# Scan systems stored in DRAM as the scan reads them, one load a step for six; the second branch's gates kept on chip

## The chip, the cores and the metric

One core of one Trainium2 chip. The metric is the time of one execution in device microseconds (us). Below, PE is TensorE, DVE is VectorE, ACT is ScalarE, POOL is GpSimd and SP is SyncE, which issues most of the DMAs. ACT issues a few DMAs too, from its own queue. In the profile, SP's transfers are DMA queue q1 and ACT's are q10.

## The reference

One layer over 256 latent tokens `x` with 256 context tokens `ctx`, all widths 2048, in float32. Two branches read the same modulated input: latent attention (MLA, 8 heads) and a bidirectional chunked gated DeltaNet (8 heads, chunks of 64 tokens). Their outputs are projected, gated, summed and projected again; a ConvGLU of width 5504 follows.

```python
(lq_a, lkv_a, lk_r, ldq, ldk, ldv, ldz, lda, ldb, lga, lgb) = split_columns(
    modulate(rmsnorm(x, norm_mix[l]), sh1, sc1) @ w_in[l])
...
m = jnp.where(strict, jnp.einsum('bhnid,bhnjd->bhnij', kb, k) * decay, 0.0)
rhs = jnp.concatenate([v * beta, kb * jnp.exp(gc)[..., None]], axis=-1)
sol = lax.linalg.triangular_solve(m + jnp.eye(c, dtype=m.dtype), rhs,
                                  left_side=True, lower=True, unit_diagonal=True)
...
def step(s, inp):
    v_new = u_c - jnp.einsum('bhcd,bhde->bhce', w_c, s)
    s_next = s * g_c + jnp.einsum('bhcd,bhce->bhde', k_c, v_new)
    o = jnp.einsum('bhcd,bhde->bhce', q_c, s) + jnp.einsum('bhcj,bhje->bhce', a_c, v_new)
...
merged = jax.nn.sigmoid(gate_mla) * (y_mla @ w_o_mla) + jax.nn.sigmoid(gate_dn) * (y_dn @ w_o_dn)
return merged @ w_out
```

What the change touches are the unit triangular 64 x 64 systems `m + I`. Each chunk has one for every head and direction. The kernel inverts them and the scan multiplies by the inverse.

## The kernel before

Nearly all time goes into matmuls of weights, which are read from DRAM once, in tiles of 128 x 1024 (512 KB, named `raw`) or 128 x 2048 (`wt`, 1 MB). For precision, each half of a tile is split into two parts: ACT casts it to `whi` (line 121) and DVE subtracts to get `wlo` (line 122); PE then runs over both. So a `raw` that lands late delays ACT's cast, DVE's subtraction and PE in turn. Over most of the program the order of PE's instructions is written out by hand; ACT, DVE and SP are put in order by a scheduler that estimates when each operand is ready.

Every DMA, on SP or on ACT, takes one of eight semaphores (`DMAHW0` to `DMAHW7`) in turn and first waits for the DMA that held the same one eight places before, whichever queue that was on. A waiting DMA holds all that stands behind it on its queue.

The stages that matter here, in order of time:

- Start (0 to some 60 us): `cv`, `sel`, `vecs`, then `xl` (the latent tokens) and `xc` (the context) in four loads each, then the adaLN weights `wt` and `raw<-in_wadab` and the first projection's `gr`. PE computes norms (`scp`, `pss`), the adaLN vectors (`amp`) and the first projections (`fp`).
- `inverse` (lines 818 to 843, about 425 to 455 us in the profile): DVE inverts the 32 x 32 diagonal blocks of all systems in the tile `ux`, and SP stores them to the DRAM tensor `Xq` in 12 stores of 32 rows of 4 KB: the first block transposed (`xt`), the first and the second.
- `off_diagonal` (lines 846 to 882, 480 to 630 us): eight steps `q` compute the 32 x 32 blocks off the diagonal from `xd<-Xq` and `uo`; ACT copies the result to `uo` and stores it to `Xo`, one store a step.
- Gates: `gate_tiles` multiplies by `wgm` and `wgd` (`gtp`), and `gate_fin` stores the tanh (`zx`) of each of 2 x 16 tiles to the DRAM tensor `Gs` from ACT's queue. `branch` loads them again, four tiles a load (`gt`), when the branch's output (`brp`) has to be gated.
- `scan` (line 1224 on, about 715 to 925 us): eight steps, each of which needs the system of its chunk in the tile `tt0` or `tt1`. `load_system` (line 1241) fills it by six loads, of 256 rows of 128 bytes each, from `Xq` and `Xo`; the quarter that stays zero was set once by POOL. PE runs the rest of the gate tiles of `wgd` and the first branch's projections (`womla`) between the steps' own products (`yp`, `sp_`, `kp`, `op`); these weights are loaded on SP's queue behind the loads of the scan.

Of the kernel before, what the change touches and what calls it, by code (L numbers as in the profile page):

```python
# [8 lines left out]
F32 = mybir.dt.float32  # L9
# [44 lines left out]
def hybrid_block(ctx: ExitStack, tc: tile.TileContext, io, dbg=None):  # L54
# [44 lines left out]
    ones = const.tile([P, 1], F32, name="ones")  # L99
    dve.memset(ones, 1.0)  # L100
    onesr = const.tile([P, P], F32R, name="onesr")
    dve.tensor_copy(onesr, ones.broadcast_to([P, P]))
# [547 lines left out]

    Xq = dram.tile([3, 32, 4, 32, 32], F32, name="Xq")
    Xo = dram.tile([32, 4, 32, 32], F32, name="Xo")
    As = dram.tile([4, P, 8, 64], F32, name="As")
# [164 lines left out]
    def inverse():  # L818
# [20 lines left out]
        for g in range(4):  # L839
            gs = slice(32 * g, 32 * g + 32)  # L840
            for n, x in enumerate((xt, X[:, 0], X[:, 1])):
                sync.dma_start(Xq[n, :, g], x[gs])
        yield 1000
        pI.close()

    def off_diagonal():
# [7 lines left out]
        def load(q):  # L854
            rs = slice(4 * q, 4 * q + 4)
            uo = pi.tile([P, 4, 32], F32, tag="uo", name="uo", bufs=2)
            sync.dma_start(uo, Uo[:, :, rs].rearrange("g j r i -> (g j) r i"))
            xd = pi.tile([P, 2, 4, 32], F32, tag="xd", name="xd", bufs=2)
            for n in range(2):
                sync.dma_start(xd[:, n], Xq[2 * n, rs].rearrange("r g j c -> (g j) r c"))  # L860
            return uo, xd
# [3 lines left out]
        for q in range(8):  # L865
# [14 lines left out]
            act.copy(uo, ip)  # L880
            act.dma_start(Xo[4 * q : 4 * q + 4].rearrange("r g c i -> (g c) r i"), uo)
            yield OC / 2
# [7 lines left out]
    def gate_fin(ps, out, fin):  # L890
        x = pz.tile([P, T], F32, tag="zx", name="zx")
        gather(ps, P, x)
        if fin is None:
            act.activation(x, x, AF.Tanh, scale=0.5)
        else:
            fin(x)
        act.dma_start(out, x)

# [285 lines left out]
    fill.finish()  # L1184
    gates = gate_tiles([("wgd", f, Gs[1, :, f], None) for f in range(KD)])
    for _ in range(4 * GD0):
# [8 lines left out]
    pd2 = pD.enter_context(pool_("pd2", 2))  # L1195
    YM = hp.tile([P, HEADS, 2, T], F32R, tag="x16", name="YM")
    yraw = pd.tile([P, HEADS, T], F32, tag="o", name="yraw")
    sync.dma_start(yraw, Ys)
# [4 lines left out]
    def branch(w, wh, f, ymat, out):  # L1203

        if f % 4 == 0:
            gt = pd2.tile([P, 4, T], F32, tag="gt", name="gt")
            sync.dma_start(gt, Gs[wh, :, f : f + 4])
            gts[wh] = gt
        W = load_w(io[w][f])
        ps = psm.tile([P, 512], F32, tag="mm", name="brp")  # L1210
# [6 lines left out]
        dve.scalar_tensor_tensor(out=ox, in0=ps[:, :T], scalar=0.5, in1=ox, op0=ALU.mult, op1=ALU.add)  # L1217
        dve.scalar_tensor_tensor(out=out, in0=gts[wh][:, f % 4], scalar=1.0, in1=ox, op0=ALU.add, op1=ALU.mult)
        yield 1300
# [4 lines left out]
    def scan():  # L1224
# [4 lines left out]
        av = ps1.tile([P, HEADS, 64], F32, name="av")  # L1229
        for n in range(2):  # L1230
            pool.memset(TTv[n], 0.0)
        half_ = [slice(0, 64), slice(64, 128)]
# [9 lines left out]
        def load_system(n):  # L1242
            st, tt = steps[n], TTv[n % 2]
            for d in range(2):
                for r, c, x in ((0, 0, Xq[1]), (32, 32, Xq[2]), (0, 32, Xo)):
                    rs, cs = slice(64 * d + r, 64 * d + r + 32), slice(c, c + 32)
                    n = 16 * d + 2 * st
                    sync.dma_start(tt[rs, :, cs], x[n : n + 2].rearrange("a g c i -> c (a g) i"))
            return tt
# [359 lines left out]
```

## Time and profile before

| | |
|---|---|
| median of 3 runs | 1796.3 us (1796.25 to 1796.43) |
| profiled execution | 1796.66 us, of which the span from the first to the last instruction is 1794.8 us |
| granted TensorE clock, mean | 0.988 |
| busy: PE, DVE, ACT, POOL | 97%, 75%, 53%, 2% of the span |
| DMA | 419.79 MB in 191493 packets, 57248 of them under 512 B |

The profile is of one execution. Its page gives the busy time of each engine, the DMA queues and the groups of instructions; the views that are asked of the trace give rows by stretch of time (busy time of each engine in it, mean granted clock, the share of the 16 DMA engines that was busy, GB/s), the instructions of one engine in order of time with the idle time ahead of each and what ended it, the waits by engine, and the chain of work that ended last. A row such as `SPq L1248` is a DMA issued by SP at line 1248.

### The profile page before, as it was taken

The numbers are of one execution on the slowest core, as the hardware profiler recorded it, in microseconds if no ns is written. First come the engines' busy times: TensorE is split into PE (matmuls) and PEld (weight loads), VectorE is DVE, ScalarE is ACT, GpSimd is POOL, SyncE is SP. The second block draws the span as 40 slices with busy tenths as digits, with TensorE's granted clock in tenths as the row PEclk, the third lists the DMA queues.
The fourth block names the chain that finished last, engine by engine and source line by source line (L and its number), as shares of the span: only waits on it lengthen the run. The fifth ranks groups of instructions, "written<-read, shape, count | busy, mean of one in ns | idle before, by whom it ended". The sixth has DMA issues, their size and how long they took to land.

```text
span 1794.8 us, 34114 instructions
## 1 busy us (share of the span) xinstructions
PE 1740.9 (97%) x12957; PEld 1504.6 (84%) x12957; DVE 1353.9 (75%) x2692; ACT 944.5 (53%) x1962; POOL 42.1 (2%) x49
## 2 busy tenths in 40 slices
PE   7999999999999999899999989999999999999999
PEld 6787888887888888687878878888888888888888
DVE  4687899879677777576789889887788888755554
ACT  3334544444567666564655546555555555544443
POOL 0000010000000000000010000000000000000000
PEclk9999999999899999999999989999999999999999
DMA  9982788773778767888957966777677777666663
GB/s 383 399 319 89 207 241 241 228 213 104 220 241 260 229 213 249 279 308 309 317 166 240 327 234 224 244 229 229 190 224 226 225 225 225 184 199 199 198 199 122
DMA packets 191493, 419.79 MB, mean 234 GB/s; under 512 B 57248, under 2 KB 97312, under 8 KB 188896
## 3 DMA queue, kind: packets, MB, share of 16 engines
q1 hardware_dynamic: 164144, 402.38, 69.0%
q10 hardware_dynamic: 27184, 15.23, 2.8%
q8 instruction: 102, 1.67, 0.4%
q14 instruction: 63, 0.52, 0.1%
HBM read 388.57 MB, written 28.84 MB: 233 GB/s over the span
## 4 chain that ended last, share of the span: by engine, by line
PE 70%; issue 10%; DMA 9%; DVE 6%; ACT 3%; POOL 1%; SPq 0%; POOLq 0%; DVEq 0%; ACTq 0%
PE fps L68 25%; PE dps L68 13%; PE mmp L68 9%; PE gtp L68 7%; PE fp L68 4%; DMA rawa<-in_wada 4%; DVE wlo L122 2%; PE brp L68 2%; DMA raw<-in_wadab 1%; PE amp L68 1%; DVE rawa L279 1%; DMA raw<-in_wgd 1%; ACT whi L121 1%; PE op L68 1%; DMA raw<-in_wz 1%
## 5 line engine op out<-in xcount | busy, mean ns | idle before, releaser
L122 DVE TENSOR_TENSOR wlo<-raw,whi 128x512 fp32r<-128x512 f32 (+1 forms) x940 | 632.6, 685 | 220.4 <-ACT whi L121 212.1
L121 ACT CAST whi<-raw 128x512 fp32r<-128x512 f32 (+1 forms) x940 | 574.3, 619 | 425.2 <-PE dps L68 113.7
L68 PE MATMUL fps<-H,whi 128*128 128x512 f32 x1376 | 475.1, 394 | 1.7 <-DVE H L1446 1.7
L68 PE MATMUL fps<-H,wlo 128*128 128x256 f32 x1376 | 372.3, 281 | 0.3 <-DVE wlo L122 0.3
L68 PEld LDWEIGHTS fps<-H,whi 128*128 128x128 f32 x1376 | 253.7, 189 | 53.3 <-issue 2.0
L68 PEld LDWEIGHTS fps<-H,wlo 128*128 128x128 f32 x1376 | 259.8, 189 | 7.8 <-DVE wlo L122 0.7
L68 PE MATMUL gtp<-h,whi 128*128 128x512 f32 x640 | 235.1, 404 | 7.4 <-ACT whi L121 7.1
L68 PE MATMUL mmp<-h,whi 128*128 128x512 f32 x640 | 227.1, 397 | 0.0
L68 PE MATMUL dps<-GB,whi 128*128 128x512 f32 (+1 forms) x595 | 195.7, 378 | 0.0
L279 DVE CUSTOM_DVE_ANT_0 rawa<-rawa,sch 128x1024 f32<-128x1024 f32 x128 | 155.8, 1220 | 45.5 <-DMA rawa<-in_wada 41.9
L68 PE MATMUL gtp<-h,wlo 128*128 128x256 f32 x640 | 176.0, 285 | 4.4 <-DVE wlo L122 4.2
L68 PE MATMUL mmp<-h,wlo 128*128 128x256 f32 x640 | 176.0, 281 | 0.6 <-DVE wlo L122 0.6
L68 PE MATMUL dps<-GB,wlo 128*128 128x256 f32 x560 | 154.1, 280 | 0.0
L68 PEld LDWEIGHTS gtp<-h,whi 128*128 128x128 f32 x640 | 121.8, 192 | 34.1 <-ACT whi L121 9.5
L68 PEld LDWEIGHTS mmp<-h,whi 128*128 128x128 f32 x640 | 119.0, 188 | 24.7 <-issue 0.4
L68 PEld LDWEIGHTS gtp<-h,wlo 128*128 128x128 f32 x640 | 122.9, 192 | 11.9 <-DVE wlo L122 7.5
L68 PEld LDWEIGHTS dps<-GB,whi 128*128 128x128 f32 x595 | 109.2, 188 | 21.1
L68 PEld LDWEIGHTS mmp<-h,wlo 128*128 128x128 f32 x640 | 120.3, 188 | 3.9 <-DVE wlo L122 1.3
L68 PEld LDWEIGHTS dps<-GB,wlo 128*128 128x128 f32 x560 | 105.1, 188 | 0.6
L68 PE MATMUL fp<-h,gh 128*128 128x256 f32 (+1 forms) x448 | 85.1, 290 | 2.5 <-ACT h L68 1.7
L68 PEld LDWEIGHTS fp<-h,gh 128*128 128x128 f32 (+1 forms) x448 | 69.4, 189 | 7.6 <-issue 4.1
L517 ACT COPY fx<-fps 128x256 f32<-128x256 f32 x86 | 31.8, 372 | 65.4 <-PE fps L68 65.3
(566 smaller groups left out, 2525.4 us busy)
## 6 DMA issues: line engine op xcount, KB each, us to landing
rawa<-in_wada SPq DMA_DIRECT2D x128, 512.0 KB, 4.7
raw<-in_wgate SPq DMA_DIRECT2D x82, 512.0 KB, 4.3
raw<-in_wval SPq DMA_DIRECT2D x82, 512.0 KB, 4.6
raw<-in_wdown SPq DMA_DIRECT2D x80, 512.0 KB, 4.3
wt<-in_wadas SPq DMA_DIRECT2D x16, 1024.0 KB, 10.8
raw<-in_wadab SPq DMA_DIRECT2D x32, 512.0 KB, 9.2
raw<-in_wgm SPq DMA_DIRECT2D x32, 512.0 KB, 4.7
raw<-in_wgd SPq DMA_DIRECT2D x32, 512.0 KB, 6.1
```

Source lines behind the costliest of these rows:

```text
L68: i = f(*a, **k)
L121: act.copy(hi, raw)
L122: dve.tensor_tensor(out=lo, in0=raw, in1=hi, op=ALU.subtract)
L279: dve.tensor_tensor_reduce(out=w, in0=w, in1=sch, scale=1.0, scalar=0.0, op0=ALU.mult, op1=ALU.add, accum_out=parts[:, h, j : j + 1])
L517: act.copy(out, ps[:M, T:])
```

## The change

- A DRAM tensor `Tt` holds every system as the scan reads it: 128 rows (64 for each direction), 16 chunks and turns, 4 heads, 64 columns. `load_system` becomes one load of 128 rows of 2 KB.
- Its zero quarter is written at the start of the program by two stores from a zeroed tile `none`, on ACT's queue: 2048 pieces of 128 bytes each.
- `inverse` no longer stores the first block untransposed to `Xq` (12 stores become 8) and stores both diagonal blocks to `Tt` in 16 stores of 512 pieces of 128 bytes, on SP.
- `off_diagonal` stores its result to `Tt` in four stores a step on SP (32 in all), where there was one to `Xo` on ACT's queue.
- POOL's two zeroings of `tt0` and `tt1` go.
- The 14 gate tiles of `wgd` that are computed inside the scan stay on chip in a new tile `gk` (14 KB a partition); their 14 stores to `Gs` go, and of the four `gt` loads of 512 KB for the second branch one of 256 KB is left.
- `dynamic_dma_scratch_size=1024` makes the room for `gk`; addresses of other tiles move.

```diff
@@ -98,6 +98,8 @@
     make_identity(nc, ident)
     ones = const.tile([P, 1], F32, name="ones")
     dve.memset(ones, 1.0)
+    none = const.tile([P, 32], F32, name="none")
+    pool.memset(none, 0.0)
     onesr = const.tile([P, P], F32R, name="onesr")
     dve.tensor_copy(onesr, ones.broadcast_to([P, P]))
     half = const.tile([P, 1], F32, name="half")
@@ -648,8 +650,10 @@
     Ud = dram.tile([4, 32, 2, 32, 32], F32, name="Ud")
     Uo = dram.tile([4, 32, 32, 32], F32, name="Uo")
 
-    Xq = dram.tile([3, 32, 4, 32, 32], F32, name="Xq")
-    Xo = dram.tile([32, 4, 32, 32], F32, name="Xo")
+    Xq = dram.tile([2, 32, 4, 32, 32], F32, name="Xq")
+    Tt = dram.tile([P, 16, 4, 64], F32, name="Tt")
+    for d in range(2):
+        act.dma_start(Tt[64 * d + 32 : 64 * d + 64, :, :, 0:32].rearrange("c s g j -> c (s g) j"), none[:32].unsqueeze(1).broadcast_to([32, 64, 32]))
     As = dram.tile([4, P, 8, 64], F32, name="As")
     conv = mid.tile([P, 24, 3], F32, name="conv")
     dve.tensor_scalar(out=conv, in0=off["dn_conv"].rearrange("p (f w) -> p f w", w=3), scalar1=0.5, scalar2=None, op0=ALU.mult)
@@ -838,8 +842,13 @@
         act.copy(xt, X[:, 0].rearrange("p c j -> p j c"))
         for g in range(4):
             gs = slice(32 * g, 32 * g + 32)
-            for n, x in enumerate((xt, X[:, 0], X[:, 1])):
+            for n, x in enumerate((xt, X[:, 1])):
                 sync.dma_start(Xq[n, :, g], x[gs])
+        for g in range(4):
+            for d in range(2):
+                for b in range(2):
+                    rs = slice(64 * d + 32 * b, 64 * d + 32 * b + 32)
+                    sync.dma_start(Tt[rs, :, g, 32 * b : 32 * b + 32].rearrange("c s j -> s c j"), X[32 * g + 16 * d : 32 * g + 16 * d + 16, b])
         yield 1000
         pI.close()
 
@@ -857,7 +866,7 @@
             sync.dma_start(uo, Uo[:, :, rs].rearrange("g j r i -> (g j) r i"))
             xd = pi.tile([P, 2, 4, 32], F32, tag="xd", name="xd", bufs=2)
             for n in range(2):
-                sync.dma_start(xd[:, n], Xq[2 * n, rs].rearrange("r g j c -> (g j) r c"))
+                sync.dma_start(xd[:, n], Xq[n, rs].rearrange("r g j c -> (g j) r c"))
             return uo, xd
 
         ahead = load(0)
@@ -878,7 +887,9 @@
                 if n == 0:
                     yield OC / 2
             act.copy(uo, ip)
-            act.dma_start(Xo[4 * q : 4 * q + 4].rearrange("r g c i -> (g c) r i"), uo)
+            for g in range(4):
+                dst = Tt[64 * (q // 4) : 64 * (q // 4) + 32, 4 * (q % 4) : 4 * (q % 4) + 4, g, 32:64]
+                sync.dma_start(dst, uo[32 * g : 32 * g + 32])
             yield OC / 2
         pI.close()
 
@@ -888,13 +899,15 @@
     pz = ctx.enter_context(pool_("pz", 3))
 
     def gate_fin(ps, out, fin):
-        x = pz.tile([P, T], F32, tag="zx", name="zx")
+        kept = isinstance(out, int)
+        x = gk[:, out] if kept else pz.tile([P, T], F32, tag="zx", name="zx")
         gather(ps, P, x)
         if fin is None:
             act.activation(x, x, AF.Tanh, scale=0.5)
         else:
             fin(x)
-        act.dma_start(out, x)
+        if not kept:
+            act.dma_start(out, x)
 
     def gate_tiles(jobs):
 
@@ -1182,7 +1195,7 @@
         pass
     inv.finish()
     fill.finish()
-    gates = gate_tiles([("wgd", f, Gs[1, :, f], None) for f in range(KD)])
+    gates = gate_tiles([("wgd", f, Gs[1, :, f] if f < GD0 else f - GD0, None) for f in range(KD)])
     for _ in range(4 * GD0):
         next(gates)
     pC.close()
@@ -1194,6 +1207,7 @@
     pd = pD.enter_context(pool_("pd", 1))
     pd2 = pD.enter_context(pool_("pd2", 2))
     YM = hp.tile([P, HEADS, 2, T], F32R, tag="x16", name="YM")
+    gk = pd.tile([P, KD - GD0, T], F32, name="gk")
     yraw = pd.tile([P, HEADS, T], F32, tag="o", name="yraw")
     sync.dma_start(yraw, Ys)
     split(yraw, YM[:, :, 0], YM[:, :, 1])
@@ -1202,10 +1216,12 @@
 
     def branch(w, wh, f, ymat, out):
 
-        if f % 4 == 0:
+        if f % 4 == 0 and (f == 0 or not wh):
             gt = pd2.tile([P, 4, T], F32, tag="gt", name="gt")
-            sync.dma_start(gt, Gs[wh, :, f : f + 4])
+            n = GD0 if wh else 4
+            sync.dma_start(gt[:, :n], Gs[wh, :, f : f + n])
             gts[wh] = gt
+        gate = gk[:, f - GD0] if wh and f >= GD0 else gts[wh][:, f % 4]
         W = load_w(io[w][f])
         ps = psm.tile([P, 512], F32, tag="mm", name="brp")
         for k in range(HEADS):
@@ -1215,7 +1231,7 @@
         ox = pd2.tile([P, T], F32, tag="ox", name="ox")
         act.activation(ox, ps[:, T:], AF.Copy, scale=0.5)
         dve.scalar_tensor_tensor(out=ox, in0=ps[:, :T], scalar=0.5, in1=ox, op0=ALU.mult, op1=ALU.add)
-        dve.scalar_tensor_tensor(out=out, in0=gts[wh][:, f % 4], scalar=1.0, in1=ox, op0=ALU.add, op1=ALU.mult)
+        dve.scalar_tensor_tensor(out=out, in0=gate, scalar=1.0, in1=ox, op0=ALU.add, op1=ALU.mult)
         yield 1300
 
     gts = {}
@@ -1227,8 +1243,6 @@
         jit = ps1.tile([P, 6, 1024], F32, name="jit")
         TTv = [ps1.tile([P, HEADS, 64], F32, name=f"tt{n}") for n in range(2)]
         av = ps1.tile([P, HEADS, 64], F32, name="av")
-        for n in range(2):
-            pool.memset(TTv[n], 0.0)
         half_ = [slice(0, 64), slice(64, 128)]
         S = ps1.tile([P, HEADS, 2, P], F32, name="S")
         steps = (4, 5, 6, 7, 0, 1, 2, 3)
@@ -1241,11 +1255,7 @@
 
         def load_system(n):
             st, tt = steps[n], TTv[n % 2]
-            for d in range(2):
-                for r, c, x in ((0, 0, Xq[1]), (32, 32, Xq[2]), (0, 32, Xo)):
-                    rs, cs = slice(64 * d + r, 64 * d + r + 32), slice(c, c + 32)
-                    n = 16 * d + 2 * st
-                    sync.dma_start(tt[rs, :, cs], x[n : n + 2].rearrange("a g c i -> c (a g) i"))
+            sync.dma_start(tt, Tt[:, 2 * st : 2 * st + 2].rearrange("p a g j -> p (a g) j"))
             return tt
 
         def load_ke(n):
@@ -1598,7 +1608,7 @@
     import concourse.bacc as bacc
     from concourse.bass_utils import run_bass_kernel_spmd
 
-    nc = bacc.Bacc("TRN2", target_bir_lowering=False, num_devices=1)
+    nc = bacc.Bacc("TRN2", target_bir_lowering=False, num_devices=1, dynamic_dma_scratch_size=1024)
     arrays = {f"in_{n}": v for n, v in host(inputs).items()}
     io = {n[3:]: nc.dram_tensor(n, v.shape, mybir.dt.from_np(v.dtype), kind="ExternalInput").ap() for n, v in arrays.items()}
     io["out"] = nc.dram_tensor("out_0", (KD, P, T), F32, kind="ExternalOutput").ap()
```

The order of the instructions on the queues changes with it. ACT at the start of the program, before (`cv`, `sel` are small inputs, `cth` and `sq` the first arithmetic):

```order
L304 DMA cv<-in_cv 128x32
L319 DMA sel<-in_sel 128x3
L307 ACT_TABLE_LOAD
L307 ACTIVATE cth<-cv 128x32
L68 ACTIVATE sq<-xl 128x4x256 x2
L68 COPY scb<-scp 128x512
```

and now:

```order
L306 DMA cv<-in_cv 128x32
L321 DMA sel<-in_sel 128x3
L656 DMA Tt<-none 2048x1x32
L309 ACT_TABLE_LOAD
L309 ACTIVATE cth<-cv 128x32
L68 ACTIVATE sq<-xl 128x4x256 x2
L656 DMA Tt<-none 2048x1x32
L68 COPY scb<-scp 128x512
```

The two zero stores stand ahead of and among the first arithmetic. SP at the same place, before, with the semaphores that each load waits for:

```order
L68 DMA xc<-in_ctxT 128x1024 [waits DMAHW0_49]
L68 DMA xl<-in_xT 128x1024 [waits DMAHW1_49]
L68 DMA xc<-in_ctxT 128x1024 [waits DMAHW2_49]
L68 DMA wt<-in_wadas 128x2048 [waits DMAHW3_49]
L68 DMA wt<-in_wadas 128x2048 [waits DMAHW4_49]
L68 DMA raw<-in_wadab 128x1024 [waits DMAHW5_49]
L68 DMA raw<-in_wadab 128x1024 [waits DMAHW6_49]
L68 DMA raw<-in_wadab 128x1024 [waits DMAHW7_49]
L68 DMA raw<-in_wadab 128x1024 [waits DMAHW0_49]
L68 DMA gr<-in_wfirst 128x864 [waits DMAHW1_49]
```

and now:

```order
L68 DMA xc<-in_ctxT 128x1024 [waits DMAHW1_49]
L68 DMA xl<-in_xT 128x1024 [waits DMAHW2_49]
L68 DMA xc<-in_ctxT 128x1024 [waits DMAHW4_49]
L68 DMA wt<-in_wadas 128x2048 [waits DMAHW5_49]
L68 DMA wt<-in_wadas 128x2048 [waits DMAHW6_49]
L68 DMA raw<-in_wadab 128x1024 [waits DMAHW7_49]
L68 DMA raw<-in_wadab 128x1024 [waits DMAHW0_49]
L68 DMA raw<-in_wadab 128x1024 [waits DMAHW1_49]
L68 DMA raw<-in_wadab 128x1024 [waits DMAHW2_49]
L68 DMA gr<-in_wfirst 128x864 [waits DMAHW3_49]
```

Semaphore 4 is now first held by the first zero store and 3 by the second (behind the first `xl`): the last `xc` load waits until the first zero store has landed, where it waited for `sel`, and the first `gr` load waits for the second zero store, where it waited for the last `xl`.

SP at the entry of the scan, before (`jit` holds the keys and values of a step, `yraw` the attention's output, `raw` are weights):

```order
L1248 DMA tt1_8862<-Xq_1824 32x8x32 x2
L1248 DMA tt1_8862<-Xo_1825 32x8x32
L1248 DMA tt1_8862<-Xq_1824 32x8x32 x2
L1248 DMA tt1_8862<-Xo_1825 32x8x32
L1207 DMA gt_8963<-Gs_4736 128x1024
L127 DMA raw_9024<-in_wgd 128x1024
L127 DMA raw_9050<-in_wgd 128x1024
```

and now:

```order
L1253 DMA jit_8901<-Vs_1822 128x1024
L1258 DMA tt1_8903<-Tt_1827 128x512
L1222 DMA gt_8990<-Gs_4740 128x1024
L129 DMA raw_9051<-in_wgd 128x1024
L129 DMA raw_9077<-in_wgd 128x1024
```

The first weight tile of the scan (`raw_9024` before, `raw_9051` now) stands behind one load of the second system instead of six.

ACT in the second step of the scan, before (`S` is the state, `y` the step's new values, `ox` a branch's product; `raw_9150` and `raw_9208` are weight tiles):

```order
L1311 ACTIVATE S_8866<-S_8866,dec_1685 128x128 x8
L1216 ACTIVATE ox_9145<-brp_9091 128x256
L1311 ACTIVATE S_8866<-S_8866,dec_1685 128x128 x4
L121 CAST whi_9152<-raw_9150 128x512
L121 CAST whi_9156<-raw_9150 128x512
L1311 ACTIVATE S_8866<-S_8866,dec_1685 128x128 x3
L1293 COPY y_9181<-yp_9182 128x512
L1293 COPY y_9181<-yp_9183 128x512
L121 CAST whi_9210<-raw_9208 128x512
L121 CAST whi_9214<-raw_9208 128x512
```

and now, where the same two weight tiles are `raw_9175` and `raw_9228`:

```order
L123 CAST whi_9177<-raw_9175 128x512
L123 CAST whi_9181<-raw_9175 128x512
L906 ACTIVATE gk_8892<-gk_8892 128x256
L1321 ACTIVATE S_8905<-S_8905,dec_1687 128x128 x9
L123 CAST whi_9230<-raw_9228 128x512
L1232 ACTIVATE ox_9170<-brp_9116 128x256
L123 CAST whi_9234<-raw_9228 128x512
L1321 ACTIVATE S_8905<-S_8905,dec_1687 128x128
L123 CAST whi_9259<-raw_9257 128x512
L123 CAST whi_9263<-raw_9257 128x512
L1321 ACTIVATE S_8905<-S_8905,dec_1687 128x128 x6
```

The casts of both tiles moved ahead: the first from behind a branch's `ox` and twelve `S` to ahead of them, the second from behind the step's `y` (which now comes after the rows shown) to that `ox`.

## The prediction

> **What bounds the kernel now.** I read the page's head and busy times first, then the busy time of each engine by stretch of time, and then, in the stretches where PE is not full, the instructions in order and the waits.
>
> ```profile
> span 1794.8 us, 34114 instructions
> PE 1740.9 (97%) x12957; PEld 1504.6 (84%) x12957; DVE 1353.9 (75%) x2692; ACT 944.5 (53%) x1962; POOL 42.1 (2%) x49
> 0.00:40.00 40.00, 30.33 (x293) 23.43 (x294) 20.54 (x38) 15.49 (x26) 2.29 (x10) 0.91 0.96 379
> 40.00:80.00 40.00, 37.69 (x434) 30.39 (x434) 28.59 (x43) 13.51 (x30) 0.00 (x0) 1.00 0.99 400
> 80.00:120.00 40.00, 40.00 (x466) 34.72 (x468) 25.91 (x40) 14.36 (x31) 0.00 (x0) 1.00 0.92 364
> 440.00:480.00 40.00, 35.46 (x243) 30.10 (x243) 25.18 (x54) 20.86 (x39) 2.02 (x2) 0.87 0.57 167
> 720.00:760.00 40.00, 32.77 (x273) 27.16 (x272) 21.68 (x42) 22.80 (x51) 0.00 (x0) 1.00 0.81 274
> 800.00:840.00 40.00, 37.76 (x429) 31.24 (x428) 29.39 (x58) 22.82 (x57) 0.00 (x0) 1.00 0.92 331
> ```
>
> PE is busy for 1740.9 of 1794.8 us, so all that any change can win without taking work from PE is 53.9 us, and this one takes none from it. In the rows by stretch the columns behind the length are PE, its weight loads, DVE, ACT and POOL, then the granted clock, the DMA share and GB/s. Two kinds of stretch bear on the change. From 0 to 80 us DMA is full (0.96 and 0.99) and PE waits for it; what is added to DMA there is paid. At 720 to 760 us, the entry of the scan, PE lacks 7.2 us though DMA has room. From 80 to 120 PE is full: a delay that enters it is kept to the end.
>
> The sum is made against the profiled execution, 1796.66 us (the span and 1.9 us outside it); the median of the runs, 1796.3, stands 0.4 us below it, and I apply the sum to the median. A difference of 0.2%, 3.6 us, is about what can be told from no change.
>
> **The zero stores at the start: +4 us.** The chain of waits (start, length, what), and the row of SP for the last `xc`:
>
> ```profile
> 3.54 10.23 DMA xc<-in_ctxT
> 13.80 12.48 DMA raw<-in_wadab
> 30.64 10.19 PE fp L68 x65
> 42.35 10.62 DMA raw<-in_wadab
> 5.70 0.77 SPq L68 DMA_DIRECT2D xc<-in_ctxT  x1
> ```
>
> Then the DMA view of 229 to 231 us, two rows; of 0 to 6 us, its GB/s in 40 slices; and the view of the tile `Xo`, its store and the time to landing:
>
> ```profile
> DMA packets 1171, 0.18 MB, mean 89 GB/s; under 512 B 1162, under 2 KB 1162, under 8 KB 1171
> q1 hardware_dynamic: 1171, 0.18, 51.6%
> GB/s 0 0 0 0 0 0 0 0 0 0 0 58 107 68 89 296 357 443 393 307 356 383 329 329 356 383 192 138 219 137 246 137 219 219 300 355 355 300 355 328
> L881 ACTq DMA_DIRECT2D Xo<-uo x8: 377/388/428, 491.4 to 624.8; - x8
> DMA to landing us min/median/max: 1.6/4.0/7.8
> ```
>
> The chain says that the start is a chain of transfers: `xc` for 10 us, `raw<-in_wadab` for 12, and again at 42. The change puts 2 x 2048 = 4096 pieces of 128 bytes into this stream. Their price is not in the trace at this place. The nearest row is a stretch of 2 us (229 to 231) with almost only stores of 128 bytes: 51.6% of 16 engines x 2 us = 16.5 us for 1171 packets, 14 ns each. That `Xo`'s 512 pieces landed in as little as 1.6 us says the same: 512/16 x 14 ns is 0.45 us. So the zeros take 4096 x 14 / 16 = 3.6 us of all engines. The upper end is from the GB/s row (0 to 6 us in 40 slices): from 3.9 to 5.1 us, while `sel`'s 128 packets of 12 bytes were under way, about 180 GB/s ran where 350 ran before: half of 1.2 us, x 16 / 128 = 75 ns a packet, and 4096 of them would be 19 us. I take 14 ns: these are stores of the same size, and `sel` is a load of other pieces. The lower end is +2: nothing in the first 80 us gives time back (0.96 and 0.99), except that the first slices run below 400 GB/s.
>
> The second part is the wait. The last `xc` (5.70) now waits for the first zero store, and behind it on SP stand `wt`, `raw<-in_wadab` and `gr`, which all of PE's chain waits for; `gr` waits for the second. At 128 packets on each engine a zero store ends about when the 7 loads issued before it do, so SP's queue runs empty and then takes some 2 us to fill again, but the rest of the zeros (64 or more packets at 14 ns, 0.9 us) runs in that hole. I add 0.4 us for it, with 0 to 4 as bounds (two holes of 2 us). ACT itself is held for two issues of 0.4 us at places where it waits for data.
>
> The Trainium skill bears on this in DMA: Bandwidth & Descriptors, Specifications: transfers under 512 bytes make the engine read, modify and write. That speaks against the change; a second pass over DRAM for each packet is the first rival below. The row of 14 ns, for stores of this very size, shows no such doubling beside what a load took, but it was no full stream.
>
> **The stores at the end of the inverse: 0.** SP's rows, and the DMA share of a stretch of small loads:
>
> ```profile
> 445.04 0.34 SPq L842 DMA_DIRECT2D Xq<-ux  x1
> 452.50 1.28 SPq L842 DMA_DIRECT2D Xq<-ux  x2
> 456.05 0.45 SPq L260 DMA_DIRECT2D rawa<-in_wada  x1
> 456.60 0.93 SPq L860 DMA_DIRECT2D xd<-Xq  x2
> 466.10 0.35 SPq L127 DMA_DIRECT2D raw<-in_wz  x1
> DMA packets 646, 0.17 MB, mean 98 GB/s; under 512 B 624, under 2 KB 624, under 8 KB 646
> 456.50:458.20 1.70, 1.70 (x11) 1.44 (x10) 0.93 (x2) 0.66 (x2) 0.00 (x0) 1.00 0.78 98
> ```
>
> SP issues 12 stores in 8.7 us (445.04 to 453.78), then `xd` and `rawa` to 457.53, and then waits until 466.10 for a weight buffer. It now issues 24 stores; 12 more at the 0.47 us of an `xd` issue (0.93 for two) are 5.6 us, which end at 463.2, inside that wait of 8.6 us. In DMA time 16 x 512 packets x 14 ns / 16 = 7.2 us come, and four stores of 128 KB go; the share there is 0.57. What is queued behind is the `raw<-in_wz` of 466.10. If the stores, which jump 16 KB from piece to piece, cost the 28 ns of the small loads (0.78 x 16 x 1.7 us = 21.2 us, less 22 large packets, over 624), they take 14.7 us, end near 464 and `xd` and `rawa` come at about 466: 0 still. Range 0 to +4, the end with both doubled again.
>
> **The off-diagonal stores: 0.** 32 issues on SP (four a step, 0.47 us each) for 8 on ACT; 1.9 us a step, over steps some 19 us apart (491.4 to 624.8 for 7 of them). Each waits for ACT's copy and holds the weights behind it on SP for that long, but weights are loaded ahead there. Range 0 to +1.
>
> **The scan: -8 us.** PE's rows at its gaps (in brackets the idle time ahead and what ended it):
>
> ```profile
> 740.03 0.49 PE L68 MATMUL gtp<-h,whi 128*128 128x512 f32 x1 [2.94 <-ACT whi L121]
> 740.76 0.38 PE L68 MATMUL gtp<-h,wlo 128*128 128x256 f32 x1 [0.23 <-DVE wlo L122]
> 753.36 0.49 PE L68 MATMUL gtp<-h,whi 128*128 128x512 f32 x1 [2.14 <-ACT whi L121]
> 759.64 0.49 PE L68 MATMUL gtp<-h,whi 128*128 128x512 f32 x1 [1.69 <-ACT whi L121]
> 847.16 0.38 PE L68 MATMUL gtp<-h,wlo 128*128 128x256 f32 x1 [1.74 <-DVE wlo L122]
> ```
>
> The groups of PE in 730 to 850 us, and SP's rows, chain and waits:
>
> ```profile
> L68 PE MATMUL gtp<-h,whi 128*128 128x512 f32 x138 | 52.0, 409 | 7.4 <-ACT whi L121 7.1
> L68 PE MATMUL gtp<-h,wlo 128*128 128x256 f32 x138 | 38.6, 290 | 4.4 <-DVE wlo L122 4.2
> 733.44 0.30 SPq L1248 DMA_DIRECT2D tt<-Xo  x1
> 734.34 5.00 DMA raw<-in_wgd
> SPq L1248 <- DMA Gs<-zx: 23.3, 6, 5.4
> 720.34 5.41 DMA yraw<-Ys
> ```
>
> And ACT's rows in the second step:
>
> ```profile
> 752.71 1.12 ACT L121 CAST whi<-raw 128x512 fp32r<-128x512 f32 x2
> 758.00 1.07 ACT L1293 COPY y<-yp 128x512 f32<-128x512 f32 x2 [3.28 <-PE yp L68]
> 758.96 2.19 ACT L121 CAST whi<-raw 128x512 fp32r<-128x512 f32 x4
> ```
>
> From 730 to 850 us PE idles 7.4 + 4.4 = 11.8 us on `gtp`. The three large gaps, each with some 0.23 us for `wlo` behind it, are 2.94 + 2.14 + 1.69 + 3 x 0.23 = 7.5 us. The first: SP held the `raw` behind the last `tt<-Xo`, which waited for a `Gs` store to land (six such waits, 23.3 us in all); it was issued at 734.34 and took 5.00 us. Both what waited and what was waited for are gone; the load stands behind one `tt1` and a `gt`, and the last semaphore it meets is that of `yraw`, landed at 725.75. Issued at 727 it lands by 733, before PE wants it at 737.1. The second and third gaps are ACT's order: the cast of 752.71 stood behind an `ox`, that of 758.96 behind `y`, which waited for PE. Both casts now stand ahead. What is late next is PE's own chain between the steps, filled with `gtp`.
>
> Of the other 4.3 us, the gap at 847.16 (1.74) follows a DVE that nothing here speeds up; of the rest I count 0.5. Also taken from DMA are 48 loads of 256 small packets (12288 x 28 ns / 16 = 21 us of engine time, against 2.1 MB now) and 3.6 MB of `Gs`, from a stretch with shares up to 0.92. Range -3 (the first gap alone) to -10.
>
> **The gates and POOL: 0.** The gates' 14 stores and 3.5 loads are counted above; POOL's two memsets had POOL's 98% idle time for cover. PE's order is the same but for small exchanges near 140 to 200 us, where PE is full.
>
> Sum: 4 + 0 + 0 - 8 + 0 = -4 us: 1796.3 - 4 = 1792.3.
>
> **Rivals.**
>
> 1. The zeros are dear: 30 ns a packet or more, as if each store also cost a small load. For it: the loads' 28 ns; against it: the stores' 14. Then 4096 x 30 / 16 = 7.7 us, and as SP's loads end long before the zero store does, `gr` waits for it with an empty queue, 2 us more: +9.7, and 1796.3 + 9.7 - 8 = 1798.0. Slower than before from +8, about 24 ns a packet; slower by 3.6 us from 38 ns; at `sel`'s 75 ns it is 1809. This is the case that the Trainium skill's rule on transfers under 512 bytes would give. Chance 0.22.
> 2. The scan's gaps come back elsewhere: a cast that moved ahead on ACT waits for its `raw` and holds `y` and `S` behind it, which the next step needs. For it: the DMA share of 0.92 at 800 to 840. Against: the DMA work taken out. Only the first gap is won: 1796.3 + 4 - 3 = 1797.3. Chance 0.16.
> 3. The 16 KB jumps stall the weights at 466: +4 more, 1796.3. Chance 0.05.
> 4. The zeros are nearly free (+1, in the slices below 400 GB/s) and the scan gives 9: 1788.3. Chance 0.13.
>
> **How the numbers follow.** The forecast, 1789 to 1795, has 0.44, and 1792.3 is its middle. The range from 1786.5 (zeros free, scan -10) to 1802 (zeros at 46 ns) takes in the rivals but for the far end of the first. Faster by over 3.6 us, below 1792.7: 0.27 of the forecast's 0.44, the cheap case's 0.13 and 0.01 besides, 0.41. Slower, above 1799.9: 0.13 of rival 1, 0.06 where 1 and 2 meet, 0.02 of 3 with either: 0.21. Within: the rest, 0.38.
>
> **What would show it.** Zeros: `raw<-in_wadab` at 42.35 in the chain should come near 46, and PE's busy time in 0 to 40 should fall from 30.33 to about 26. Scan: no `tt` wait for `Gs`, the first `raw<-in_wgd` issued near 727, 720 to 760 with PE over 38. Inverse: `raw<-in_wz` still issued some 21 us after the first `Xq`. The prediction fails if the zeros take more than 20 ns each, or if the gaps at 737 to 760 return behind other waits.

## The result and the profile after

The changed kernel takes 1790.9 us (median of 15 runs) against 1796.26 for the kernel before, run beside it: a ratio of 0.9969, with a 95% interval from 0.9959 to 0.9978, so 5.4 us or 0.3% faster. The profiled execution of it took 1789.27 us, at the faster end of its runs, with a span of 1787.5.

The page, and the busy time by stretch of the same clock times as before:

```profile
span 1787.5 us, 34086 instructions
PE 1741.8 (97%) x12957; PEld 1507.3 (84%) x12957; DVE 1354.9 (76%) x2692; ACT 942.8 (53%) x1962; POOL 42.8 (2%) x48
0.00:40.00 40.00, 28.09 (x253) 20.97 (x254) 15.67 (x31) 14.54 (x25) 2.36 (x11) 0.84 0.96 345
440.00:480.00 40.00, 34.31 (x360) 28.27 (x359) 22.72 (x49) 19.14 (x38) 2.08 (x2) 0.96 0.51 105
720.00:760.00 40.00, 39.55 (x315) 33.82 (x314) 24.99 (x48) 23.86 (x53) 0.00 (x0) 1.00 0.92 344
800.00:840.00 40.00, 39.73 (x465) 34.25 (x458) 31.45 (x63) 24.08 (x60) 0.00 (x0) 1.00 0.97 363
```

PE's busy time is what it was; its idle time fell from 53.9 to 45.7 us. A stretch of clock time compares different work once one kernel lags, so I followed milestones instead. In the view of the tile `yp`, PE's first product of the scan, and of `osp`, the first after it, before and then after (count, durations, first and last start):

```profile
L68 PE MATMUL yp<-jit,tt x32: 269/269/320, 731.0 to 731.9; 64*64 64x128 f32 x32
L68 PE MATMUL osp<-ones,osq x128: 170/170/191, 916.5 to 919.7; 128*32 128x1 f32 x128
```

```profile
L68 PE MATMUL yp<-jit,tt x32: 269/269/320, 736.4 to 737.3; 64*64 64x128 f32 x32
L68 PE MATMUL osp<-ones,osq x128: 170/170/213, 908.9 to 912.2; 128*32 128x1 f32 x128
```

The scan starts 5.4 us late and its end comes 7.5 us early: the stretch from the one to the other shrank from 188.7 to 175.8 us, by 12.9. The chain of waits of the start tells where the 5.4 came from:

```profile
1.67 13.65 DMA Tt<-none
15.34 4.46 DMA xc<-in_ctxT
35.63 10.26 PE fp L68 x65
47.42 9.26 DMA raw<-in_wadab
```

The `fp` that began at 30.64 begins at 35.63: 5.0 us. Of the rest, 0.4 was added between there and the scan. So the change costs 5 us at the start and wins 13 in the scan, of which 7.3 are left in the profiled execution and 5.4 in the medians.

In the scan, the groups of PE from 730 to 850 us that stood at 7.4 and 4.4 us of idle time:

```profile
L68 PE MATMUL gtp<-h,whi 128*128 128x512 f32 x163 | 59.0, 399 | 0.0
L68 PE MATMUL gtp<-h,wlo 128*128 128x256 f32 x163 | 43.9, 280 | 0.0
```

And PE's whole stretch from the first `yp` to the last `osp`, before and after:

```profile
731.00:919.70 188.70, 175.60 (x2007) 148.00 (x2008) 130.32 (x269) 108.43 (x262) 0.00 (x0) 0.99 0.86 299
```

```profile
736.40:912.20 175.80, 173.25 (x2008) 148.55 (x2008) 131.63 (x272) 106.40 (x263) 0.00 (x0) 1.00 0.86 306
```

Idle time fell from 13.1 to 2.6 us, 10.5; the other 2.4 us are matmuls that take less time themselves. Most of that is one dip of the granted clock in the kernel before, behind the gap at 847.16:

```profile
848.00:851.50 3.50, 3.50 (x13) 3.01 (x12) 2.05 (x4) 0.00 (x0) 0.00 (x0) 0.52 0.80 217
```

PE is busy through all of it, but at 0.52 of full speed, so about 3.5 x 0.48 = 1.7 us of the 2.4 are lost there. In the changed kernel the granted clock is 1.00 over the whole scan.

### The profile page after: what moved, and what is told of

Read it like the earlier page. It is cut to its first block, busy times and chain, and to the rows that moved or that the text cites. A ratio compares the mean times of both kernels' runs of the same rounds, so it can differ in the third digit from the quotient of the medians.

```text
span 1787.5 us, 34086 instructions
## 1 busy us (share of the span) xinstructions
PE 1741.8 (97%) x12957; PEld 1507.3 (84%) x12957; DVE 1354.9 (76%) x2692; ACT 942.8 (53%) x1962; POOL 42.8 (2%) x48
## 4 chain that ended last, share of the span: by engine, by line
PE 77%; issue 10%; DMA 6%; DVE 4%; ACT 2%; POOL 1%; SPq 1%; POOLq 0%; ACTq 0%; DVEq 0%
PE fps L68 26%; PE dps L68 13%; PE mmp L68 12%; PE gtp L68 8%; PE fp L68 4%; PE brp L68 2%; DMA rawa<-in_wada 2%; DVE wlo L124 1%; PE amp L68 1%; PE vps L68 1%; PE tp L68 1%; DMA Tt<-none 1%; PE kp L68 1%; PE op L68 1%; PE kps L68 1%
## 5 line engine op out<-in xcount | busy, mean ns | idle before, releaser
L68 PE MATMUL gtp<-h,whi 128*128 128x512 f32 x640 | 230.6, 398 | 0.0
```

Source lines behind the costliest of these rows:

```text
L68: i = f(*a, **k)
```

## The experiments

Twelve kernels were run, each timed in five rounds beside the kernel before. The ratios are to that kernel. The diffs are excerpts; `...` marks what is left out.

**Which half of the change wins the scan: the gates or the systems?** `gates_only` is the kernel before with `gk`; `systems_only` is the changed kernel with the gate tiles in DRAM again.

```diff
# gates_only, on the kernel before
...
+        x = gk[:, out] if kept else pz.tile([P, T], F32, tag="zx", name="zx")
+        if not kept:
             act.dma_start(out, x)
...
# systems_only, on the changed kernel
-    gates = gate_tiles([("wgd", f, Gs[1, :, f] if f < GD0 else f - GD0, None) for f in range(KD)])
+    gates = gate_tiles([("wgd", f, Gs[1, :, f], None) for f in range(KD)])
...
```

> The kernel before, with only the 14 gate tiles kept on chip (their stores and the loads that read them back are gone); systems are stored and loaded as before, no zero stores. In the trace after, all of PE's 11.8 us of waits on gtp in the scan are gone. Theory A (the weight loads of the scan waited behind system loads that waited for a gate store's semaphore): the gates alone win most of it, 8 to 11 us, so 1785 to 1788 us. Rival B (six loads a step of small packets take SP's and the DMA engines' time): the gates alone win 0 to 3 us, 1793 to 1796.

> The changed kernel, but with the 14 gate tiles stored to DRAM and read back as before. It pays the zero stores at the start (5.0 us by the first fp: 35.63 against 30.64) and the stores at the inverse (theory A: 2). Theory A: one load a step still waits for gate stores, the scan wins 3 to 4 us: 1796.3 + 7 - 3.5 = 1800. Rival B: the six loads were what cost, the scan wins 8 to 13: 1790 to 1795.

Measured: `gates_only` 1.0001 (0.9985 to 1.0018), no change; `systems_only` 0.9987 (0.9972 to 1.0003). From `gates_only`, PE's groups in 730 to 860 us:

```profile
L68 PE MATMUL gtp<-h,whi 128*128 128x512 f32 x153 | 60.3, 425 | 6.5 <-ACT whi L121 6.2
L68 PE MATMUL gtp<-h,wlo 128*128 128x256 f32 x154 | 44.5, 300 | 3.4 <-DVE wlo L122 3.3
```

The 14 gates that are computed inside the scan are not stored here, and 9.9 of the 11.8 us of waits are still there. But two of the 16 gate tiles are computed at the scan's entry, and every kernel here still stores them. In `gates_only` the first weight load of the scan still stands behind a DMA that waits for the second of these stores. SP's wait at 722 to 745, the load, and PE's first gap:

```profile
SPq L1211 <- DMA Gs<-zx: 2.6, 1, 2.6
735.81 0.85 SPq L127 DMA_DIRECT2D raw<-in_wgd  x2
741.64 0.80 PE L68 MATMUL gtp<-h,whi 128*128 128x512 f32 x1 [2.50 <-ACT whi L121]
```

The load was asked for 2.7 us after the first `yp` (733.07); in the kernel before it was 3.3 us after. In the changed kernel it is asked for 3.9 us ahead of the first `yp`, and the first gap is gone:

```profile
732.53 2.20 SPq L129 DMA_DIRECT2D raw<-in_wgd  x2
```

So `gates_only` is no test of the first gap. From `systems_only`, the milestones and one of SP's waits in 700 to 930 us:

```profile
L68 PE MATMUL yp<-jit,tt x32: 268/270/321, 738.9 to 739.7; 64*64 64x128 f32 x32
L68 PE MATMUL osp<-ones,osq x128: 169/170/192, 910.9 to 914.1; 128*32 128x1 f32 x128
SPq L129 <- DMA Gs<-zx: 9.2, 5, 3.5
```

Its scan takes 175.2 us, as short as the changed kernel's, though its weight loads wait for gate stores; there too the first weight load is asked for ahead of the first `yp`, by 4.8 us. Theory A, that the gate stores' semaphores made the gaps, falls for the stores inside the scan. The scan's gain is from the systems. This verdict rests on the scan: by its total, `systems_only` is not told from the kernel before, and why its scan starts 2.5 us later than the changed kernel's was not taken apart.

**Small packets, or six loads?** `tt_six` loads the same whole rows in six pieces.

```diff
...
-            sync.dma_start(tt, Tt[:, 2 * st : 2 * st + 2].rearrange("p a g j -> p (a g) j"))
+            for lo, hi in ((0, 32), (32, 48), (48, 64), (64, 96), (96, 112), (112, 128)):
+                sync.dma_start(tt[lo:hi], Tt[lo:hi, 2 * st : 2 * st + 2].rearrange("p a g j -> p (a g) j"))
...
```

> The changed kernel, with each system loaded in six loads of whole rows (2 KB pieces, the same bytes) instead of one. The two kernels run before this tell that the gates alone win nothing and the systems alone win the scan. ACT's order falls back here: the scheduler puts the weight casts of the scan behind y, ox and S, as in the kernel before. Theory O (the gaps come from where the casts stand on ACT, which follows from how many DMAs SP has to issue ahead of the weights): the gaps of 2 to 3 us return and it is 8 to 11 us slower than the changed kernel, 1799 to 1802. Rival P (the small packets held the DMA engines): as fast as the changed kernel, 1790 to 1792.

Measured: 1801.56 us, 1.0034 (1.0021 to 1.0047), 10.7 us slower than the changed kernel. PE's groups in 730 to 860, then ACT's and SP's rows in the second step:

```profile
L68 PE MATMUL gtp<-h,whi 128*128 128x512 f32 x170 | 63.2, 407 | 6.8 <-ACT whi L123 6.6
L68 PE MATMUL gtp<-h,wlo 128*128 128x256 f32 x169 | 47.3, 290 | 3.6 <-DVE wlo L124 3.5
```

```profile
750.62 0.33 SPq L129 DMA_DIRECT2D raw<-in_wgd  x1
762.19 0.36 ACT L1232 ACTIVATE ox<-brp 128x256 f32<-128x256 f32 x1
763.33 1.12 ACT L123 CAST whi<-raw 128x512 fp32r<-128x512 f32 x2
768.61 1.07 ACT L1304 COPY y<-yp 128x512 f32<-128x512 f32 x2 [3.56 <-PE yp L68]
769.57 3.23 ACT L123 CAST whi<-raw 128x512 fp32r<-128x512 f32 x6
```

The bytes and the packets are those of the changed kernel, and the gaps are back: it is not the small packets. The weights asked for at 750.62 were cast only at 763.33, behind the branch's `ox`, and the next behind `y`; no wait for a DMA stands ahead of these two casts. The first gap (2.37 us) is back in another way: SP waits for the entry's gate store ahead of the first weight load, which is asked for 1.9 us after the first `yp` (740.9), and the cast waits for it. SP's wait at 722 to 745, then ACT's row:

```profile
SPq L1222 <- DMA Gs<-zx: 4.4, 1, 4.4
748.64 2.41 ACT L123 CAST whi<-raw 128x512 fp32r<-128x512 f32 x4 [0.51 <-DMA raw<-in_wgd]
```

That the scheduler counts on the weights later when SP has six loads to issue, and so puts the casts further back on ACT, is the likely reason for the order; no run shows what it reckoned with.

**The order of the casts alone.** `before_ttact` is the kernel before with its six loads a step on ACT's queue, which moves the casts ahead; `gates_ttact` adds `gk`.

```diff
...
-                    sync.dma_start(tt[rs, :, cs], x[n : n + 2].rearrange("a g c i -> c (a g) i"))
+                    act.dma_start(tt[rs, :, cs], x[n : n + 2].rearrange("a g c i -> c (a g) i"))
...
```

> The kernel before, with the 48 small system loads of the scan (six a step, 128-byte pieces) issued from ACT's queue instead of SP's, and nothing else. The bytes, the packets and the gate stores stay. In ACT's order the weight casts of the scan now stand ahead of y, of most of S and of the branch's ox, as in the changed kernel. Theory O (the gaps are the casts' place): the gaps at the entry of the scan go, 8 to 13 us faster than before, 1783 to 1788. Rival P (the small packets or the number of loads hold the DMA engines and the semaphores): 0 to 3 us, 1793 to 1796. Rival E (ACT, held by the issues and by the gate stores' semaphores, is late with its casts): slower than before.

> As before_ttact, with the 14 gate tiles kept on chip too (which alone won nothing). ACT then has no gate stores in the scan whose semaphores could hold it. Theory O: as fast as before_ttact or up to 2 us faster, 1782 to 1787; it pays neither zero stores nor stores at the inverse. Rival E: 1790 or more.

Measured: `before_ttact` 0.9992 (0.9976 to 1.0007), `gates_ttact` 0.9974 (0.9959 to 0.9989). The groups of PE with idle time in `before_ttact`, 725 to 920 us:

```profile
L68 PE MATMUL brp<-YM,whi 128*128 128x512 f32 x125 | 48.2, 417 | 3.1 <-ACT whi L121 3.1
L68 PE MATMUL kp<-S,jit 128*64 128x128 f32 x224 | 14.4, 276 | 0.9 <-DVE S L1324 0.8
L68 PE MATMUL yp<-r,tt 64*64 64x128 f32 x224 | 10.3, 297 | 5.0 <-DVE r L1283 5.0
L68 PE MATMUL sp__9530<-y,jit 64*128 64x128 f32 x8 | 1.4, 297 | 1.6 <-ACT y L1293 1.6
```

Not one wait on `gtp` is left, as theory O had it; but about as much waits in other places, 4.7 us on ACT and 5.8 us on DVE. The time, 1794.45 us, is neither theory O's nor slower than before, as rival E had it; it is the number of rival P, under which the `gtp` gaps would have stayed. This kernel moves two things at once: the casts stand ahead, and the first weight load is asked for at 727.63, before its first `yp` (729.6). So it shows that the gaps go with both, not which of the two closes which gap. What share of the new waits is ACT's issuing and what its new order was not taken apart either.

`gates_ttact`, at 1792.23 us, is faster than the kernel before but misses theory O's 1782 to 1787; rival E's 1790 or more holds. Whether keeping the gates wins anything is open: `gates_only` shows nothing, and with the systems changed (0.9969 against 0.9987) or the loads on ACT (0.9974 against 0.9992) it is 0.0018 either time, inside the intervals.

What these kernels show together is this. The second and third gap are the place of the casts on ACT: in the kernel before, `gates_only` and `tt_six` the casts stand behind `ox`, `S` or `y` with no wait for a DMA. The first goes with the weight load that is asked for after the scan has begun, behind a wait for a gate store. In the kernel before, `gates_only`, `tt_six` and the two kernels with zeros of the next part, the load comes 0.9 to 3.3 us after the first `yp`, and `gtp` has a gap of 1.8 to 2.9 us; in the changed kernel and `systems_only` it comes ahead of it, and there is none. One load a step for six mends both.

**The start.** `before_zeros` adds only the two zero stores to the kernel before; `before_zeros_big` stores the same bytes in pieces of 4 KB; `zeros_late` is the changed kernel with the stores moved.

```diff
# before_zeros: as in the change.  before_zeros_big:
...
+        act.dma_start(Tt[64 * d : 64 * d + 64], none[64 * d : 64 * d + 64])
...
# zeros_late, in inverse() behind the load of ux
...
+        for d in range(2):
+            osync.dma_start(Tt[64 * d + 32 : 64 * d + 64, :, :, 0:32].rearrange("c s g j -> c (s g) j"), none[:32].unsqueeze(1).broadcast_to([32, 64, 32]))
```

> The kernel before, with only the two zero stores of the start added (to a DRAM tensor that nothing reads). Theory A (delay of the start is kept to the end): the 5.0 us that the first fp came later in the trace after, 1801. Rival C (part is made good before the scan): +2 to +3, 1798 to 1799.

> The kernel before, with two stores of zeros of the same bytes at the same places, but in pieces of 4 KB: 4 packets on each engine instead of 128. Theory W (the cost is the last xc load waiting until all 128 small packets an engine have taken their turn between SP's packets): the store lands early, only its DMA time of 0.5 MB at 400 GB/s, 1.3 us, is left: 1797 to 1798. Rival L (any store that takes a semaphore there costs its 5 us): 1801.

> The changed kernel, with the two zero stores moved from the start of the program to behind the load of ux for the inverse, on SP, where DMA is 0.2 to 0.4 busy. Theory A (the start is held by DMA and a delay there is kept to the end): 5 us faster than the changed kernel, 1786. Rival C (the delay of the start is made good somewhere before the scan): the same as the changed kernel, 1791.

Measured: 1.0027 (1.0007 to 1.0047), 1.0000 (0.9981 to 1.0019) and 0.9941 (0.992 to 0.9963; 1783.78 us). The tile `fp` in the kernel before, in `before_zeros` and in `before_zeros_big`:

```profile
L68 PE MATMUL fp<-h,gh x448: 277/280/529, 29.6 to 140.1; 128*128 128x256 f32 x128, 128*96 128x256 f32 x22
```

```profile
L68 PE MATMUL fp<-h,gh x448: 277/280/529, 34.9 to 144.3; 128*128 128x256 f32 x128, 128*96 128x256 f32 x22
```

```profile
L68 PE MATMUL fp<-h,gh x448: 277/280/527, 31.3 to 140.5; 128*128 128x256 f32 x128, 128*96 128x256 f32 x22
```

In small pieces the zeros delay the first `fp` by 5.3 us, in large ones by 1.7. So most of the delay comes from the number of packets, and at most 1.7 us from their bytes and from the place of the stores. Whether the 5 us are kept to the end `before_zeros` alone does not tell: its ratio amounts to 4.8 us, and its interval, 1.3 to 8.4 us, takes in theory A's 5 and rival C's 2 to 3. Moved to where DMA has room, the zeros cost nothing that shows: `zeros_late` is 7 us faster than the changed kernel by the medians and 5 by the ratios, theory A's 5 us, where rival C had none.

**The inverse.** After the change SP is long in the stores, by its rows, by its wait there, and by ACT's wait and PE's gap behind it:

```profile
457.23 18.61 SPq L851 DMA_DIRECT2D Tt<-ux  x16
478.89 0.38 SPq L129 DMA_DIRECT2D raw<-in_wz  x1
SPq L851 <- DMA Zs<-zx: 7.1, 1, 7.1
ACT whi L123 <- DMA raw<-in_wz: 13.2, 2, 12.4
483.69 0.39 PE L68 MATMUL vps<-whi,kvn 128*128 128x256 f32 x1 [3.53 <-DVE V L124]
```

Four kernels tried to win the 3.5 us back. `inv_spread` puts four of the stores into each of the first four off-diagonal steps; `zl_spread_uoact` does so with the zeros late and the off-diagonal stores on ACT; `zl_half` is `zeros_late` with half of the 16 stores on ACT; `zl_d2d` stores half of them later, from `Xq`.

```diff
# inv_spread, in off_diagonal(), and ux allocated in pool pc
...
+            if q < 4:
+                diagonal(q)   # the four stores of g = q
...
# zl_spread_uoact, as well
...
-                sync.dma_start(dst, uo[32 * g : 32 * g + 32])
+                act.dma_start(dst, uo[32 * g : 32 * g + 32])
...
# zl_half, in inverse()
...
-                    sync.dma_start(Tt[rs, :, g, 32 * b : 32 * b + 32]...
+                    (act if b else sync).dma_start(Tt[rs, :, g, 32 * b : 32 * b + 32]...
...
# zl_d2d, in off_diagonal(), b = 1 only
...
+            sync.dma_start(Tt[64 * d + 32 : 64 * d + 64, :, g, 32:64].rearrange("c s j -> s c j"), Xq[1, 16 * d : 16 * d + 16, g])
```

> The changed kernel, with the 16 stores of the diagonal blocks moved from the end of the inverse into the first four steps of the off-diagonal stage, four a step (ux stays allocated until then). In the trace after SP is in these stores from 457.2 to 475.9, the xd and weight loads behind them are late, ACT waits 12.4 us for raw<-in_wz and PE 3.5 us. Theory A (that gap is a loss of its own): 2 to 3 us faster than the changed kernel, 1788 to 1789. Rival C (the stage has slack and makes it good): the same, 1791. Worse than 1791.5 if the stores now hold the weights of the off-diagonal steps.

> The changed kernel with the zero stores on SP behind the load of ux, the 16 diagonal stores in the first four off-diagonal steps, and the off-diagonal stores on ACT's queue, so that SP does not wait for ACT's copy (57.3 us of such waits in the trace of inv_spread, and PE gaps of 7 to 11 us behind the weights that stood after them). Theory D: with that wait off SP the spread is free and wins the 3.5 to 4.4 us gap at 480: 1780 to 1782, against 1783.8 for the zeros alone. Rival E (ACT pays 32 issues of some 0.4 us ahead of its casts): 1784 to 1788.

> zeros_late with half of the 16 diagonal stores on ACT's queue. Theory F (the weight load raw<-in_wz of the trace after stood behind 18.6 us of stores on SP, 7.1 of them a wait for the semaphore of a store on ACT's queue; half the stores end before it is due): the PE gap of 4.4 us at 478.84 in zeros_late closes, 1779 to 1781. Rival E (ACT is held by eight stores while PE waits for its casts): 1784 or more.

> zeros_late with only the first block's 8 diagonal stores at the end of the inverse; the second block's 8 are copied later from Xq to Tt, DRAM to DRAM, one in each off-diagonal step. Theory F (SP's 18.7 us of stores ahead of raw<-in_wz make the PE gap of 4.4 us at 478.84): SP is through some 9 us earlier, raw<-in_wz is issued before 472, the gap closes and ACT is not held as in zl_half: 1779 to 1781 against 1783.8. Rival C (the stage makes that gap good later): 1783 to 1785. Rival E (the copies hold weights in the off-diagonal steps, as the spread stores did): 1790 or more.

Measured: 1.0162 (1.0138 to 1.0187), 1.009 (1.0072 to 1.0108), 0.9922 (0.9896 to 0.9947) and 1.0045 (1.003 to 1.0059). None is faster than `zeros_late` beyond the intervals, and three are slower. From `inv_spread` a PE gap, and SP's wait in 476 to 600 us; from `zl_half` its PE gap; from `zl_d2d` SP's wait in 440 to 660:

```profile
502.49 0.79 PE L68 MATMUL qps<-qan__4750,whi 128*128 128x512 f32 x1 [10.57 <-ACT whi L123]
SPq L898 <- ACT uo L895: 57.3, 4, 16.1
```

```profile
459.83 1.52 PE L68 MATMUL kps<-kvn,whi 128*128 128x512 f32 x2 [8.69 <-ACT kvn L123]
```

```profile
SPq L890 <- ACT uo L887: 33.1, 6, 7.7
```

In `inv_spread` and `zl_d2d` the off-diagonal stores wait longer on SP for ACT's copy, with the weights behind them: 57.3 and 33.1 us in all, against 11.0 in the changed kernel (480 to 640). Rival E of `zl_d2d` holds, by its number and by this wait. In `zl_half` the gap at 480 is gone, and one of 8.7 us has come where ACT holds a cast behind eight stores that it issues (449.5 to 458.9). That is rival E's mechanism, but its number was 1784 or more and 1783.46 came, with an interval that takes in theory F's 1781 too, so the two stay undecided; the kernel is not told from `zeros_late`. In `zl_spread_uoact` the off-diagonal stores are off SP, and at 1813.88 us it is still slower: SP now waits 23.3 us for such stores to land (440 to 640), with weights behind. Theory D falls.

## Why the prediction was right, and which terms were off

The direction and the sum (1792.3 against 1790.9) came out, and so did what decides it: a loss at the start by the zeros' packets, and a larger gain in the scan by gaps that close. That the sum came out so near is in part luck. Its two terms were both too small, the loss by 1 us and the gain by 5; and the profiled execution of the changed kernel gained 7.3 us on the other profile where the medians gained 5.4.

- **The zeros, +4: measured +5.0.** The price of a packet was right: on ACT's queue 4416 packets of the first 60 us took 6.0% of 16 engines, 13 ns each, where 14 was taken.

```profile
q10 hardware_dynamic: 4416, 0.54, 6.0%
GB/s 0 212 236 317 297 328 404 407 392 252 115 235 344 421 410 401 407 421 418 411 440 436 410 407 391 412 410 407 425 432 421 406 418 405 410 412 431 400 406 425
```

That is 3.3 us. The wait was put at 0.4 and is the other 1.7: SP's queue ran dry behind the last `xc`, as the first zero store landed only 13.65 us after its issue, and the rest of the zeros did not fill the hole. In the GB/s of the first 60 us, in slices of 1.5 us, it is the 252, 115 and 235 about 15 us. The first rival, packets at 30 ns, is refuted. The Trainium skill (DMA: Bandwidth & Descriptors, Specifications) says that transfers under 512 bytes miss line rate, as the engine reads, modifies and writes. The trace agrees on the rate: 128 bytes in 13 ns are 9.8 GB/s for one engine, where SP's queue moved 21.50 MB in 92.0% of the same 60 us, 24.3 GB/s for each. Whether each packet is also read first can't be told from a time alone; that the same bytes cost more in small pieces than in large ones, the two kernels with zeros show.

- **The inverse, 0: a PE gap of 3.53, of which little was left at the scan.** The step that failed is the end of SP's stores, put at 463: they ended at 475.84, as one of them waited 7.1 us for a `Zs` store that ACT issued only at 468.06. Without that wait they would have ended at 468.7, on a clock that ran 6.6 us later by then. A packet of these stores took 16.6 ns (41.9% of 16 engines for 6480 packets at 459 to 475), not the 28 of the doubtful case (for which 8192 packets make 14.3 us, not 14.7; nothing hung on it). `raw<-in_wz` came 27.3 us after the first `Xq`, not 21. The row of that `Xq`, and a gap of the kernel before that matters next:

```profile
451.64 0.34 SPq L846 DMA_DIRECT2D Xq<-ux  x1
521.67 0.60 PE L68 MATMUL ks<-ones,ksq 128*32 128x1 f32 x32 [3.75 <-DVE km L1022]
```

From the start to the scan the delay grew from 5.0 to 5.4 us only. Between the first `Xq` and the scan PE idles 12.4 us before and 14.6 after, 2.2 more, as this 3.75 us is 1.57 after; and PE is busy 3.4 us less, at a granted clock of 0.99 for 0.97. Why the clock was higher there is not shown, so that little of the gap was left is in part chance.
- **The off-diagonal stores, 0: right where they stood.** SP waits 11.0 us for ACT's copy there, and PE has no gap behind it. `inv_spread` and `zl_d2d` show how little stood behind that: with more stores in these steps and longer waits they are 13 us and more slower than the changed kernel.
- **The scan, -8: measured -12.9, beyond its own end of -10.** The reason given for the first gap, a weight load behind a system load that waits for a gate store, stands: the load is asked for at 732.53, which is 727.1 on a clock without the 5.4 us, and before PE needs it. Only that the gate store itself is gone was wrong; the changed kernel still stores that tile, but the DMA that waits for it (a `jit` load, 3.7 us) now stands behind the weights. The reason given for the second and third, the place of the casts on ACT, holds too, as `tt_six` shows. What was too small is the rest: of 4.3 us besides the three gaps 0.5 was counted, and 10.5 us of idle time went in all; the 1.74 at 847.16 that was to stay went too. And the matmuls themselves took 2.4 us less, of which the clock dip behind that gap is about 1.7: no step had that.
- **Rival 2, casts that wait for their weights and hold `y` behind them: there, but small.** ACT's casts of the changed scan wait 14.1 us for `raw<-in_wgd`, where they waited 7.4 before, but PE waits only 1.0 us for `y` behind them.

Of the signs that were named, `raw<-in_wadab` came at 47.42 for 46, 720 to 760 has 39.55 us of PE for over 38, and no `tt` load waits for `Gs`. PE's busy time in 0 to 40 fell to 28.09 only, where 26 was forecast.

The two fastest kernels are the changed one with its zeros moved, `zeros_late` and `zl_half`, at 1783.8 and 1783.5 us, 0.6 to 0.8% below the kernel before; they are not told apart.

## What to carry to other kernels

Where a scheduler sets the order, the gain or loss of one load fewer is in what it moves on other queues: read the order of the engine that the bound waits for, and test it with a kernel that has the same bytes in as many loads as before. See that an experiment takes away the very instruction that the theory names: `gates_only` took 14 gate stores away and left the one that the first weight load waits behind. Thousands of small packets belong in a stretch where DMA has room, never at a start that waits for data, and the load that meets their semaphore can pay more than their time (here 5.0 us for 3.3). A store that waits for an engine should not stand ahead of loads on the same queue; several attempts to make room by moving stores cost more than they won.

## What the runs showed of the hardware

With the same bytes, 4 KB pieces delayed the start by 1.7 us and 128-byte pieces by 5.3. Stores of 128 bytes took 13 ns of an engine each at the start.

Matmuls of one shape take longer where the granted clock is lower. In `gates_only`, behind its gap of 2.50 us:

```profile
741.60:747.80 6.20, 6.16 (x18) 4.95 (x19) 6.03 (x10) 2.79 (x5) 0.00 (x0) 0.50 1.03 417
```

There `gtp<-h,whi` takes 0.63 us, against a median of 0.39 at a clock of 1.00. Such dips are a large part of why its mean is 407 to 425 ns in the kernels with gaps and 399 in the changed one. The dips seen in the scans came behind gaps of 1.7 to 2.5 us of PE, but gaps of 1.7 to 2.9 us without a dip are there too, so that gaps make the clock fall is not shown.
